# Starting addresses in SBUF: the buffers of the transposing DMAs move to multiples of 128 bytes

## The chip, the cores and the metric

The kernel runs on one core of one Trainium2 chip. The metric is device time in microseconds (us), the median of several runs of the whole program. The profile is of one further execution of it. The span is the time from the first to the last instruction in that execution.

## The reference: one hybrid encoder layer

The input `x` has 2048 tokens of width 1024, and there are 256 memory tokens. One layer is computed:

```
h    = rms_norm(x, norm_pre_w)
proj = h @ w_in          # aq (8 heads), ak, av (2 heads), bqkv, ba, bb, mq, z
y_a  = softmax attention of 8 query heads over 2 key/value heads, 2048 x 2048, 2-D rotary
y_b  = gated DeltaNet, forward and backward, 4 heads, after a short convolution
y_m  = softmax attention of 4 heads into the 256 memory tokens
mix  = concatenate([y_a, y_b, y_m]) * silu(z)
out  = x + rms_norm(mix @ w_out, norm_post_w)
```

All of it is float32 at the interface. The change concerns the softmax attention `y_a` and `y_m`: there, `P = softmax(scores)` has queries in the partitions and keys along the free axis, and the product `P @ V` needs `P` with keys in the partitions, so `P` is transposed.

## The kernel before

The work stands in stages that follow each other, with some overlap.

1. **Projections** (0 to about 880 us): weights are loaded through tiles called `wraw` and split into two fp16 parts, a high part and a remainder; the normalised tokens `hT` are kept in the same way. Queries, keys, values, gates and the DeltaNet inputs go to scratch tensors in HBM.
2. **DeltaNet scan** (about 880 to 1360 us): chunk by chunk, with gate projections as filler for TensorE.
3. **Attention** (about 1360 to 2310 us): 64 attention units of 256 queries of one head, each of two blocks of 128 queries, and 8 memory units of one block. That makes 136 blocks.
4. **Output projection** (about 2310 to 2650 us).

One attention block goes as follows. TensorE computes scores `sa` of 128 queries against 2048 keys, VectorE (DVE) takes their maximum `mxa`, ScalarE (ACT) exponentiates into `Pa`, and `high` and `low` make two fp16 parts of the scaled result side by side in one tile `hl` (named `hla` for attention blocks and `hlm` for memory blocks; 128 partitions by 8192 bytes, three buffers): the high part by ACT, the remainder by DVE for 1536 keys and by GpSimd (POOL) for 512. Then one DMA of 1 MB, issued on the queue of SyncE (SP), transposes `hl` into half of a tile `PT`, SBUF to SBUF. There are four `PT` tiles of 128 partitions by 16384 bytes, used in turn: `PT0` and `PT1` in the pool `hT`, `PT2` and `PT3` in the pool `late`. The value product `pva` (for memory units `pvm`) reads `PT` and `V` on TensorE. Its result is multiplied by a gate `gaa` that is loaded from HBM, and stored to `mix` in HBM.

The pool `hT` has six rooms of 16384 bytes per partition under the tag `B16`. In turn they hold `wraw`, `mT`, `hT0` to `hT3`, and later `K0`, `K1`, `V`, `M`, `PT0`, `PT1`, `mhl` and `wo`. The pools `wp`, `zp`, `at`, `bp`, `op` and those of the early stages lie behind it in SBUF, so that where `hT` ends sets where they begin. The pool `const`, which holds a few scale factors, lies before it.

During attention, ACT, DVE, TensorE and the sync queue run in the order in which the program was written. All loads and stores of this stage go through SP's queue, in one order with the transposes.

Of the kernel before, what the change touches and what calls it, by code (L numbers as in the profile page):

```python
# [11 lines left out]
F32 = mybir.dt.float32  # L12
F32R = mybir.dt.float32r
BF16 = mybir.dt.bfloat16
F16 = mybir.dt.float16
# [7 lines left out]
S = 2048  # L23
D = 1024
NMEM = 256
# [3 lines left out]
KC = D // 128  # L29
# [8 lines left out]
def hybrid_layer(ctx: ExitStack, tc: tile.TileContext, t: dict, out, dbg=None):  # L38
# [40 lines left out]
    const = ctx.enter_context(tc.tile_pool(name="const", bufs=1))  # L79
# [35 lines left out]
    ssq = const2.tile([128, 4, TB], F32, name="ssq")  # L115
    vmax = const2.tile([128, TB], F32, name="vmax")
    mvmax = const2.tile([128, 2], F32, name="mvmax")
    vs, vcs, mvs, mvcs, hs_, hcs = (const.tile([128, 1], F32, name=n) for n in ("vs", "vcs", "mvs", "mvcs", "hs", "hcs"))
    gcs = const.tile([128, 8], F32, name="gcs")
    gate_cs = [gcs[:, i:i + 1] for i in range(8)]  # L120

# [25 lines left out]
    def load_w(srcs, width, fac=(1.0,), fetch=None):  # L147


        n = wcount[0]  # L150
        wcount[0] += 1
        room = hpool.tile([128, 2, 4, width], F32, tag="B16", name="wraw", bufs=6)
        raws = [room[:, half] for half in range(2)]
        for half in range(2):
            for ap_to, ap_from in srcs(raws[half], half):
                (fetch or wdma)(ap_to, ap_from)
        pool, tag, bufs = (wpool, "whb", 2) if wpool is not None and n % 3 == 1 else (wp, "whl", 4)
        parts = [pool.tile([128, 2, 4, width], F16, tag=tag, name="wparts", bufs=bufs) for _ in range(2)]

        def small(name, dt=F32, pool=const2, bufs=4):  # L160
            return pool.tile([128, 1], dt, tag=name, name=f"{name}{n}", bufs=bufs)

        ss = [small(f"wss{i}") for i in range(2)]
        for half in range(2):
            A.activation(parts[half][:, 0].bitcast(BF16), raws[half], AF.Square, accum_out=ss[half])
        sb, y, e, sc = small("wsb", BF16), small("wy"), small("we", I32), small("wsc")
        V.tensor_tensor(sb, ss[0], ss[1], op=ALU.add)
        ps = tp_ps(f"wss{n}", (128, 1))
        T.matmul(ps, onesb, sb, start=True, stop=True)
        V.tensor_scalar(y.bitcast(I32), ps.bitcast(I32), -0.5, 1597463007.0, op0=ALU.mult, op1=ALU.add)  # L170
        V.tensor_scalar(e, y.bitcast(I32), 0x7f800000, None, op0=ALU.bitwise_and)
        V.tensor_scalar(sc.bitcast(I32), e, 1.0, float(14 << 23), op0=ALU.mult, op1=ALU.add)
        V.tensor_scalar(y.bitcast(I32), e, -1.0, float(240 << 23), op0=ALU.mult, op1=ALU.add)
        cs = [small("wc1", bufs=2)] * (len(fac) - 1) + [small("wc0", pool=const)]
        for c, f in zip(cs, fac):
            V.tensor_scalar(c, y, hcs, f, op0=ALU.mult, op1=ALU.mult)
        G.tensor_scalar(raws[1], raws[1], sc, None, op0=ALU.mult)
        A.activation(parts[0][:, 0], raws[0], AF.Copy, scale=sc)
        A.copy(parts[1][:, 0], raws[1])
        V.scalar_tensor_tensor(parts[0][:, 1], raws[0], sc, parts[0][:, 0], op0=ALU.mult, op1=ALU.subtract)  # L180
        G.tensor_tensor(parts[1][:, 1], raws[1], parts[1][:, 0], op=ALU.subtract)
        return [(w[:, 0], w[:, 1]) for w in parts], cs
# [3 lines left out]
    hpool = ctx.enter_context(tc.tile_pool(name="hT", bufs=1))  # L186
# [9 lines left out]
    def tp_ps(name, shape=(128, 512)):  # L196
        return ps1.tile(list(shape), F32, tag="tp", name=name, bufs=4)

    hT = []
# [48 lines left out]
    def load_group(segs, fetch=None, fac=(1.0,)):  # L248

        def src(raw, half):  # L250
            o = 0
            for c0, n in segs:
                yield raw[:, :, o:o + n], t["w_in"][0, 512 * half:512 * half + 512, c0:c0 + n].rearrange("(k p) c -> p k c", p=128)
                o += n
        return load_w(src, sum(n for _, n in segs), fac, fetch)
# [12 lines left out]
    with tc.tile_pool(name="s0", bufs=1) as p:  # L268
# [15 lines left out]

        wmem = p.tile([128, D], F32, tag="wn", name="wmem")
        wpre = p.tile([128, D], F32, tag="wn", name="wpre")
        mTt = hpool.tile([128, 2, KC, NMEM], F32R, tag="B16", name="mT", bufs=6)
        mT = [mTt[:, i] for i in range(2)]
        xs, hm = [], []
        for j in range(2):  # L290
# [58 lines left out]
        for g in range(4):  # L349
# [2 lines left out]
                wav, (avcs,) = load_group([(1280, 256), (3072, 16)], dma)  # L352
            mem_group(g, wg)
            wg = nxt
        hT.extend(hpool.tile([128, 2, KC, 512], F16, tag="B16", name=f"hT{b}", bufs=6).rearrange("p i k c -> i p k c") for b in range(4))
        hs = {}

        def tok_norm(tb):
# [285 lines left out]
                    (attention_loads, attention_slots)[b]()  # L644

    def slot(name, shape, dt=F32R):
        return hpool.tile(shape, dt, tag="B16", name=name, bufs=6)

    def late_slot(name, shape, dt=F32R):

        return late.tile(shape, dt, tag="L16", name=name, bufs=2)

    at = {}

    def attention_loads():

        at["k"] = [slot("K0", [128, 2, S])]
        at["q0"] = wp.tile([128, 2, QW], F32R, tag="wraw", name="qa0_0", bufs=1)
        dma(at["q0"], qT_d[0, :, :, 0:QW])
        for k in range(4):  # L660
            dma(at["k"][0][:, :, k * 512:(k + 1) * 512], kT_d[0, :, :, k * 512:(k + 1) * 512])

    def attention_slots():
        at["v"] = slot("V", [128, 2, TB, 256], F16)
        at["PT"] = [slot(f"PT{i}", [128, 2, 2, 16, 128], F16) for i in range(2)]
# [108 lines left out]
    with tc.tile_pool(name="s3a", bufs=1) as sv0:  # L774
        p = rows
# [24 lines left out]
        for hp in range(2):  # L800
            p = (sv0, sv1)[hp]
# [222 lines left out]
    late = ctx.enter_context(tc.tile_pool(name="late", bufs=1, side="right"))  # L1024
    ps2 = ctx.enter_context(tc.tile_pool(name="ps2", bufs=1, space=PSUM))
    p5 = ExitStack()
    p = p5.enter_context(tc.tile_pool(name="at", bufs=1))
# [7 lines left out]
    class Block:  # L1035
# [62 lines left out]
            V.reciprocal(sm[:, 2:3], sm[:, 2:3])  # L1098

        def high(self):  # L1100
            hl = self.hl = p.tile([128, 2, S], F16, tag="hl", name=f"hl{self.nm}", bufs=3)
            P = self.P.rearrange("p a c -> p (a c)")
            if self.u["mem"]:
                A.copy(hl[:, 0], P)
            else:
                A.activation(hl[:, 0], P, AF.Copy, scale=self.sm[:, 2:3])
            n = self.u["n"]
            if n in (2, 3) and len(PT) == n:
                PT.append(late_slot(f"PT{n}", [128, 2, 2, 16, 128], F16))
            self.pt = PT[n % 4][:, self.qb]  # L1110
# [136 lines left out]
    for i in range(len(blocks) + LAG + 1):  # L1247
# [31 lines left out]
        for tb in range(2):  # L1279
            n = i - len(blocks) - 2 * tb  # L1280
# [38 lines left out]
    with ExitStack() as es:  # L1319
        p = es.enter_context(tc.tile_pool(name="op", bufs=1))  # L1320
        wo.append([late_slot(f"wo{i}_2", [128, 4, D]) for i in range(2)])
        wo.append([p.tile([128, 4, D], F32R, name=f"wo{i}_3") for i in range(2)])

# [98 lines left out]
```

## Time and profile before

| | us |
|---|---|
| median of 3 runs (lowest to highest) | 2656.08 (2654.11 to 2661.66) |
| the profiled execution, its own time | 2652.8 |
| its span | 2650.6 |
| TensorE busy in the span | 2419.5 (91%) |
| VectorE busy | 1763.9 (67%) |
| ScalarE busy | 1258.9 (47%) |
| GpSimd busy | 691.4 (26%) |

The mean granted clock of TensorE is 0.975. The profiled execution is 3.3 us below the median of the runs, and 2.2 us of its time lie outside the span. Lines of the profile name an operation as output, an arrow, and inputs, without buffer numbers; nearly all operations have one source line, since a helper records them, so they are told apart by the names of tiles.

### The profile page before, as it was taken

Reading aid. Unit: us, or ns where it says so; the run is one execution under the profiler, and the core shown is the slowest. Engines: PE = TensorE matmul, PEld = TensorE weight load, DVE = VectorE, ACT = ScalarE, POOL = GpSimd, SP = SyncE. Lnnn points to the kernel's source line nnn. Section 1 sums busy time; section 2 is a strip of 40 time slices with the busy share of each in tenths; the row PEclk is TensorE's granted clock in tenths of the full one; section 3 lists DMA queues with packets and bytes.
Section 4 is the critical chain, followed back from the end, with each engine's and each line's share of the span. In section 5 each row is a group of like instructions: output and inputs, shape, how many; then the busy total and the mean of one; then the engine's idle time right before and its main releaser. Section 6 shows DMA issues by size and latency. Waiting matters only on the chain.

```text
span 2650.6 us, 43177 instructions
## 1 busy us (share of the span) xinstructions
PE 2419.5 (91%) x15970; PEld 1739.9 (66%) x15978; DVE 1763.9 (67%) x3423; ACT 1258.9 (47%) x2495; POOL 691.4 (26%) x572
## 2 busy tenths in 40 slices
PE   7899999999989899989997888888888988999998
PEld 6788965555544366666556666666666766788887
DVE  6677769999568545455447787777877877542222
ACT  4633335444432255555546666666666666421110
POOL 2154331111203210210214444344444333200000
PEclk9999999999999999999999999999999999999999
DMA  6433333234586667678669999999999999953331
GB/s 212 150 118 123 116 101 104 72 116 130 195 256 159 204 191 215 209 236 235 205 192 228 223 229 223 227 228 220 217 217 208 211 202 203 210 167 98 97 97 54
DMA packets 867730, 470.49 MB, mean 178 GB/s; under 512 B 640576, under 2 KB 809920, under 8 KB 867264
## 3 DMA queue, kind: packets, MB, share of 16 engines
q1 hardware_dynamic: 853792, 420.54, 65.7%
q0 software_dynamic: 13728, 47.19, 5.3%
q8 instruction: 126, 2.06, 0.3%
q14 instruction: 84, 0.69, 0.1%
HBM read 201.82 MB, written 123.21 MB: 123 GB/s over the span
## 4 chain that ended last, share of the span: by engine, by line
PE 26%; issue 11%; DMA 8%; POOL 8%; DVE 3%; ACT 1%; SPq 1%; POOLq 0%; DVEq 0%; ACTq 0%
PE o L51 12%; PE sa L51 4%; PE z L51 3%; POOL hla L51 3%; PE pva L51 3%; POOL Pa L51 2%; DMA PT<-hla 2%; DMA gaa<-gate 2%; POOL Pm L51 1%; DMA PT<-hlm 1%; PE pvm L51 1%; DVE mxa L51 1%; DMA xx<-bx 1%; DVE hla L51 1%; DMA n<-NI 1%
## 5 line engine op out<-in xcount | busy, mean ns | idle before, releaser
L51 PEld LDWEIGHTS <-wparts 128*128 128x128 f16 x3072 | 292.8, 98 | 326.8 <-issue 18.4
L51 PE MATMUL pva<-PT,V 128*128 128x256 f16 x3072 | 394.7, 280 | 97.6 <-DMA PT<-hla 91.1
L51 PE MATMUL sa<-K,qa 128*128 128x512 f32 x1536 | 435.3, 420 | 9.8 <-ACT Pm L51 5.1
L51 PEld LDWEIGHTS <-V 128*128 128x128 f16 x3072 | 287.3, 100 | 205.7 <-issue 109.6
L51 DVE TENSOR_REDUCE mxa<-sa 128x1 f32<-128x1024 f32 x256 | 309.6, 1217 | 138.2 <-PE sa L51 135.7
L51 ACT ACTIVATE Pa<-sa,mxa 128x1024 f32<-128x1024 f32 x256 | 282.6, 1110 | 242.0 <-DVE mxa L51 167.0
L51 PE MATMUL z<-hT,wparts 128*128 128x512 f16 x1536 | 371.9, 383 | 0.3
L51 PE MATMUL o<-wo,mhl 128*128 128x512 f32 x1416 | 325.1, 391 | 1.2 <-ACT wo L51 0.6
L51 PEld LDWEIGHTS sa<-K,qa 128*128 128x128 f32 x1536 | 281.6, 197 | 65.7 <-ACT Pm L51 6.5
L51 PEld LDWEIGHTS o<-wo,mhl 128*128 128x128 f32 x1416 | 265.3, 188 | 60.5 <-ACT wo L51 1.1
L51 DVE SCALAR_TENSOR_TENSOR hla<-Pa,sma,hla 128x1536 f16<-128x1536 f32 x128 | 284.5, 2222 | 14.8 <-ACT hla L51 14.5
L51 ACT ACTIVATE hla<-Pa,sma 128x2048 f16<-128x2048 f32 x128 | 256.1, 2001 | 58.7 <-DMA PT<-hla 50.1
L51 PE MATMUL b<-hT,wparts 128*128 128x512 f16 x1152 | 256.9, 379 | 0.5 <-ACT xb L51 0.5
L51 POOL TENSOR_TENSOR Pa<-Pa,sma 128x512 f32<-128x512 f32 x128 | 133.0, 1039 | 472.6 <-ACT hla L51 464.1
L51 PEld LDWEIGHTS <-hT 128*128 128x128 f16 x2304 | 227.0, 99 | 31.9 <-ACT hT L51 1.2
L51 PE MATMUL q<-wparts,hT 128*128 128x256 f16 x1920 | 215.6, 274 | 0.0
L51 POOL TENSOR_TENSOR hla<-Pa,hla 128x512 f16<-128x512 f32 x128 | 195.4, 1527 | 8.9
L51 POOL TENSOR_SCALAR wraw<-wraw,wsc 128x1024 f32<-128x1024 f32 (+1 forms) x22 | 68.1, 3097 | 335.7 <-DVE wy L51 224.1
L51 DVE TENSOR_TENSOR mhl<-mr,mhl 128x2048 fp32r<-128x2048 f32 (+1 forms) x16 | 35.1, 2192 | 179.7 <-ACT mhl L51 179.5
L51 DVE SCALAR_TENSOR_TENSOR y<-xb,convw,y 128x512 f32<-128x512 f32 x192 | 147.3, 782 | 1.5
L51 ACT CAST mhl<-mr 128x2048 fp32r<-128x2048 f32 (+1 forms) x16 | 29.2, 1825 | 228.3 <-PE o L51 214.4
L77 POOL DMA_DIRECT2D gate<-zg x64 | 35.5, 555 | 368.8 <-DVE zg L51 190.9
(302 smaller groups left out, 3244.3 us busy)
## 6 DMA issues: line engine op xcount, KB each, us to landing
xx<-bx SPq DMA_DIRECT2D x64, 512.0 KB, 4.8
wraw<-in_w_in POOLq DMA_DIRECT2D x42, 512.0 KB, 5.4
qT<-qo SPq DMA_DIRECT2D x32, 512.0 KB, 3.1
qa<-qT SPq DMA_DIRECT2D x64, 256.0 KB, 3.8
gate<-zg POOLq DMA_DIRECT2D x64, 256.0 KB, 4.0
NI<-nit SPq DMA_DIRECT2D x32, 512.0 KB, 3.5
mr<-mix SPq DMA_DIRECT2D x13, 1024.0 KB, 6.0
x<-in_x SPq DMA_DIRECT2D x16, 512.0 KB, 4.9
```

Of the source, the lines that this page charges most:

```text
L51: ins = f(*args, **kw)
L77: nc.gpsimd.dma_start(to, of)
```

## The change

The pools take an alignment for the tiles that share rooms with `PT` (the tag `B16`), for `late_slot`, and for `hl`. Six tiles of one float per partition in `const` become six columns of one tile.

```diff
-    vs, vcs, mvs, mvcs, hs_, hcs = (const.tile([128, 1], F32, name=n) for n in ("vs", "vcs", "mvs", "mvcs", "hs", "hcs"))
+    scales = const.tile([128, 6], F32, name="scales")
+    vs, vcs, mvs, mvcs, hs_, hcs = (scales[:, i:i + 1] for i in range(6))
 ...
-        room = hpool.tile([128, 2, 4, width], F32, tag="B16", name="wraw", bufs=6)
+        room = hpool.tile([128, 2, 4, width], F32, tag="B16", name="wraw", bufs=6, align_bytes=128)
 ...
-        mTt = hpool.tile([128, 2, KC, NMEM], F32R, tag="B16", name="mT", bufs=6)
+        mTt = hpool.tile([128, 2, KC, NMEM], F32R, tag="B16", name="mT", bufs=6, align_bytes=128)
 ...
-        hT.extend(hpool.tile([128, 2, KC, 512], F16, tag="B16", name=f"hT{b}", bufs=6).rearrange("p i k c -> i p k c") for b in range(4))
+        hT.extend(hpool.tile([128, 2, KC, 512], F16, tag="B16", name=f"hT{b}", bufs=6, align_bytes=128).rearrange("p i k c -> i p k c") for b in range(4))
 ...
-        return hpool.tile(shape, dt, tag="B16", name=name, bufs=6)
+        return hpool.tile(shape, dt, tag="B16", name=name, bufs=6, align_bytes=128)
 ...
-        return late.tile(shape, dt, tag="L16", name=name, bufs=2)
+        return late.tile(shape, dt, tag="L16", name=name, bufs=2, align_bytes=128)
 ...
-            hl = self.hl = p.tile([128, 2, S], F16, tag="hl", name=f"hl{self.nm}", bufs=3)
+            hl = self.hl = p.tile([128, 2, S], F16, tag="hl", name=f"hl{self.nm}", bufs=3, align_bytes=128)
```

What comes of it in the built program: every engine and every queue has the same instructions in the same order, with the same waits and the same semaphore updates; only the names of the six scale factors and the addresses differ. The addresses (bytes within a partition) go as follows; the last two columns give the place of the start behind the last multiple of 256.

| tiles | address before | after | before, mod 256 | after, mod 256 |
|---|---|---|---|---|
| `hl`, first of three buffers | 171744 | 171776 | 224 | 0 |
| `PT0` | 82464 | 82304 | 32 | 128 |
| `PT1` | 33312 | 33152 | 32 | 128 |
| `PT2` | 196576 | 196480 | 224 | 128 |
| `PT3` | 212960 | 212864 | 224 | 128 |
| `K0`, `K1`, `V`, `M`, `wraw`, `hT0` to `hT3` | -160 each | | 32 | 128 |
| `xx`, `it`, `gaa`, `qa`, `oo`, `zg` (pools behind `hT`) | -64 each | | 32 | 224 |
| `qo`, `mo` | -64 each | | 224 | 160 |
| `kt`, `sv` (in the DeltaNet inputs) | -64 each | | 96 | 32 |
| `ku` | -64 | | 32 | 224 |
| `nit` | 0 | | 96 | 96 |

The three `hl` buffers are 8192 bytes apart, and the halves of a `PT` tile too.

## Prediction

> **What bounds the kernel now.** I first read the busy time by stage (engines' busy time, then granted clock, DMA share, GB/s; the stages are those of the text above).
>
> ```profile
> core 0: us, PE busy (x) PEld busy (x) DVE busy (x) ACT busy (x) POOL busy (x), PEclk, DMA share, GB/s
> 1381.00:1900.00 519.00, 439.63 (x2807) 342.99 (x2805) 406.48 (x515) 332.80 (x479) 218.62 (x155) 0.95 1.11 224
> 1900.00:2310.00 410.00, 361.20 (x2267) 280.21 (x2266) 310.91 (x384) 255.85 (x300) 163.05 (x125) 0.96 1.08 209
> 2310.00:2650.00 340.00, 331.22 (x1444) 270.25 (x1442) 108.46 (x202) 51.38 (x56) 0.00 (x0) 1.00 0.34 107
> 0.00:1381.00 1381.00, 1287.45 (x9457) 846.41 (x9466) 938.01 (x2325) 618.84 (x1662) 309.73 (x293) 0.98 0.55 168
> ```
>
> Outside attention TensorE is busy 93% to 97% of the time, and no transposing DMA runs there. In attention (929 us, the first two rows) it is busy 800.8 us and idle 128. So 128 us is the most that anything done to the transposes could bring. Next, the answer on the tile `PT`: durations as least/median/greatest in ns, then who waits for it.
>
> ```profile
> L1122 SPq DMA_TRANSPOSE PT<-hla x128: 4685/5318/10240, 1381.1 to 2288.5; - x128
> L1122 SPq DMA_TRANSPOSE PT<-hlm x8: 4870/4964/5514, 1450.3 to 1878.2; - x8
> ...
> who waited for it (us, times):
>   PE pva L51: 91.1, 41
>   PEld L51: 85.8, 26
>   ACT hla L51: 52.3, 35
>   PE pvm L51: 19.2, 5
> ...
> DMA to landing us min/median/max: 6.7/7.4/12.3
> ```
>
> TensorE's matmuls wait 91.1 + 19.2 = 110.3 us for transposes, most of its idle time, in 46 of 136 cases. So the transposes do bound this stage, and the change is aimed at the right place. The question is what sets their pace. The first two rows are not the transfer: they are how long the issuing instruction holds SP's queue. At the medians that is 128 x 5.318 + 8 x 4.964 = 720 us of the 907 us between the first and the last. The order of time on SP's queue (start, duration) shows what fills the rest:
>
> ```profile
> 1756.28 6.25 SPq L1122 DMA_TRANSPOSE PT<-hla  x1
> 1762.58 4.95 SPq L1122 DMA_TRANSPOSE PT<-hlm  x1
> 1767.62 0.54 SPq L51 DMA_DIRECT2D mix<-gaa  x1
> 1768.26 4.90 SPq L1122 DMA_TRANSPOSE PT<-hla  x1
> 1773.26 0.55 SPq L51 DMA_DIRECT2D qa<-qT  x1
> 1773.91 4.96 SPq L1122 DMA_TRANSPOSE PT<-hla  x1
> ```
>
> Instructions stand with gaps of about 0.1 us. An ordinary load of the same 1 MB holds the queue for a thirteenth of that (row from the answer on `mr`, the output projection's input):
>
> ```profile
> L51 SPq DMA_DIRECT2D mr<-mix x16: 370/370/436, 2280.7 to 2580.6; - x16
> ```
>
> Is the hold the time that SP needs to issue the pieces, or is it held back by the transfer? If by the transfer, and if the transfer is slow because of its addresses, the change helps. Three short stretches inside single transposes tell this apart:
>
> ```profile
> 1406.90:1410.40 3.50, 3.50 (x28) 2.97 (x26) 2.62 (x6) 2.56 (x3) 1.85 (x2) 1.00 1.27 290
> 1491.90:1494.40 2.50, 2.50 (x19) 1.96 (x17) 1.94 (x5) 1.21 (x3) 0.56 (x1) 1.00 1.28 290
> 1764.00:1768.00 4.00, 4.00 (x31) 3.29 (x29) 3.15 (x5) 2.92 (x3) 1.00 (x1) 1.00 1.17 218
> ```
>
> The last is the ordinary pace, 218 GB/s: 1.0486 MB / 218 GB/s = 4.81 us, which is the hold of 4.685 to 4.96 us. The first two come late in transposes whose transfer was held up at its start while SP went on issuing; there the engines catch up at 290 GB/s, 3.62 us for 1 MB. Every `hl` buffer in this run starts at 224 behind a multiple of 256, these included. So the addresses of before allow 290 GB/s, and the ordinary 218 is set ahead of the data, at SP. How many pieces SP issues is shown by the packets of the stage:
>
> ```profile
> DMA packets 619683, 201.84 MB, mean 217 GB/s; under 512 B 565216, under 2 KB 617312, under 8 KB 619616
> ```
>
> Fewer than 565216 / 136 = 4156 pieces a transpose, so 4096 of 256 bytes make up the 1 MB: SP needs about 4.8 us / 4096 = 1.2 ns for each.
>
> **The change part by part.** *The transposes.* Source starts go from 224 to 0 behind a multiple of 256, destination starts from 32 (`PT0`, `PT1`) and 224 (`PT2`, `PT3`) to 128. The number of instructions, waits and pieces stays. Two prices are possible. If SP's issuing sets the hold, and a piece costs SP the same at any address, the gain is 0. If the address sets it, the bound on the other side is the pace of 290 GB/s or better: 4.81 - 3.62 = 1.19 us a transpose, 136 x 1.19 = 162 us of SP's time, more than the 110.3 us that TensorE waits, so all of these go and no more: -110.3. I take 0, since the stretches at 290 were reached with the old addresses. Where I am least sure is whether SP's 1.2 ns a piece itself depends on the address; no row shows a transpose at another source start, so the lower end stays.
>
> The Trainium skill, page "DMA: Bandwidth & Descriptors", section "How a descriptor splits into AXI transactions", speaks for a gain: a read starts at the 256-byte boundary below its start, and the bytes fetched ahead of it still cost beats of 32 bytes. By that a piece of 256 bytes at 224 costs 8 + 7 = 15 beats and an aligned one 8; with the 435 GB/s that the same page's specifications give as the fabric's ceiling, this would allow, as an estimate, 435 x 8 / 15 = 232 GB/s before. The ordinary 218 would fit; the 290 of the two stretches does not, so here the measurement decides against it. The sum by that rule would be -110.3 instead of 0.
>
> *The other rooms of `hT`* (`wraw`, `K`, `V`, `M`, `hT0` to `hT3`) go from 32 to 128, *and the tiles of the later pools* from 32 to 224 or from 224 to 160. Whether a plain DMA cares is bounded by transfers of equal size that start at different places before (size, us from issue to landing):
>
> ```profile
> qT<-qo SPq DMA_DIRECT2D x32, 512.0 KB, 3.1
> NI<-nit SPq DMA_DIRECT2D x32, 512.0 KB, 3.5
> bx<-kt SPq DMA_DIRECT2D x32, 256.0 KB, 2.3
> bx<-ku SPq DMA_DIRECT2D x16, 256.0 KB, 2.5
> ```
>
> The first pair starts at 224 and 96, the second at 96 and 32. The differences are 0.4 us in favour of 224 and 0.2 us against 32, with no order in them. All four are stores; they are the nearest rows, since the loads of these stages all start at 32. So the price of a move is between -0.4 and +0.4 us a transfer; I take 0, the middle, because the two pairs contradict each other. Where it would matter is where an engine waits for such loads (the waits: us in total, times, longest; behind them the loads, from the same view as the pairs above):
>
> ```profile
> DVE xx L51 <- DMA xx<-bx: 76.6, 47, 3.3
> DVE gaa L51 <- DMA gaa<-gate: 31.9, 15, 5.5
> ```
>
> ```profile
> xx<-bx SPq DMA_DIRECT2D x64, 512.0 KB, 4.8
> gaa<-gate SPq DMA_DIRECT2D x64, 128.0 KB, 3.7
> ```
>
> These are 47 + 15 = 62 waits, and both tiles go from 32 to 224: 62 x 0.4 = 25 us either way at the most.
>
> *The scale factors.* Six tiles become columns 4 bytes apart. Same writes, same reads, same waits: 0, with nothing that has to cover it. *Engines reading moved tiles:* matmuls on `PT` and the writers of `hl` keep shape and order. Half of the value products of before read a `PT` that starts at 32 and half one at 224 (`pvm` likewise), and they show no two prices: the median lies within 4 ns of the least.
>
> ```profile
> L51 PE MATMUL pva<-PT,V x3072: 269/273/437, 1397.9 to 2305.1; 128*128 128x256 f16 x192
> L51 PE MATMUL pvm<-PT,mv x192: 272/273/437, 1457.0 to 1890.5; 128*128 128x256 f16 x192
> ```
>
> I take 0 there; if each of the 3264 moved by 1 ns, the next whole number of the record, it would be 3 us either way.
>
> The sum is 0, with unknowns of -110.3 (transposes), +-25 (plain DMAs) and +-3 (matmuls). On the profiled execution that gives 2652.8 us. The median of the three runs is 3.3 us above it, and the change is measured against such medians, so I forecast 2656 us. A change of 0.3%, 8 us, is about what a measurement of this kernel can tell from none: the three runs differ by 7.6.
>
> **The rivals.** *A, the address sets the pace after all.* The hold then falls from 4.8 to 3.6 us or lower, SP's queue is free for a sixth of the stage, and the 110.3 us of waits go: 2656 - 110 = 2546 us; next late would be `mxa` waiting for `sa`, that is TensorE itself. For it: hold and transfer are nearly equal in length, and the order of the queue is packed. Against: 290 GB/s with the old addresses. The rule of the Trainium skill told above, from its page "DMA: Bandwidth & Descriptors", would lead to this case.
>
> *B, only the tail shrinks.* The median hold of 5.318 lies above the least, 4.685, since transposes run into transfers ahead of them. If aligned reads clear these faster, so that the hold falls to its least value, 0.63 us a transpose, it counts where TensorE waits: 46 x 0.63 = 29 us, so 2627 us. For it: the DMA share of 1.08 to 1.11 in the stage, so that engines are rarely idle. Against: the share counts overlapping packets (1.28 at 290 GB/s, 1.17 at 218), so that it shows no queue.
>
> *C, slower: the tiles pushed to 224 load later.* 62 waits on `xx` and `gaa` grow by up to 0.4 us: 2656 + 25 = 2681 us. It decides, against no change, from 8 / 62 = 0.13 us a transfer on. For it: loads of `xx` and `gaa` end waits of DVE on the path. Against: the store that starts at 224 (`qo`) is the quicker of its pair.
>
> **How the numbers follow.** No change 0.54; A 0.18 (the source of every transpose moves, and the stage is bound by them, but the rates contradict it); B 0.15; C 0.13. B and A end faster, C slower: faster 0.33, same 0.54, slower 0.13. The likeliest case alone lies in 2648 to 2664. The range for 8 in 10 must reach B on one side and into C on the other, and leaves A out: 2590 (between A and B, since a smaller part of A is as likely as all of it) to 2672 (C at two thirds of its price).
>
> **What would show it.** In the profile after, the row of `PT<-hla` should again have 4.7 and 5.3 us as least and median, with TensorE's waits near 110 us, and the window's GB/s near 217. A least hold below 4.5 us would show A; a median near 4.7 with the same least, B. Landings of `xx` (4.8 us) and `gaa` (3.7) up by over 0.13 us would show C. The forecast is wrong first of all if SP's time for a piece depends on where it starts.

## The result and the profile after

The changed kernel takes 2580.08 us (median of 4 runs, 2576.74 to 2586.11) against 2655.56 us of the kernel before (the three runs of the table above and one more): a ratio of 0.9714, with a 95% interval of 0.969 to 0.9738. A run more than 1.5% above the fastest of its kernel is left out of the ratios; there is one such run here, in experiment 5. The forecast was 2656, so the kernel gained some 75 us that the forecast did not see, and the time lies below its range. The profiled execution has a span of 2576.6 us, 74.0 less than before.

Busy time by stage, in the columns shown before:

```profile
core 0: us, PE busy (x) PEld busy (x) DVE busy (x) ACT busy (x) POOL busy (x), PEclk, DMA share, GB/s
1383.00:1900.00 517.00, 459.26 (x2984) 360.07 (x2983) 440.39 (x548) 355.14 (x505) 244.72 (x167) 0.96 1.11 241
1900.00:2233.00 333.00, 322.88 (x2094) 253.54 (x2093) 288.57 (x349) 231.40 (x273) 149.87 (x114) 0.99 1.08 233
2233.00:2573.00 340.00, 333.14 (x1442) 271.25 (x1440) 108.79 (x203) 51.40 (x56) 0.00 (x0) 0.99 0.33 105
0.00:1383.00 1383.00, 1286.28 (x9463) 844.92 (x9464) 937.15 (x2325) 618.43 (x1662) 308.84 (x293) 0.98 0.55 168
```

The stages ahead of and behind attention are as long as they were, within some 3 us. Attention went from 929 to 850 us, and TensorE's idle time in it from 128.2 to 67.9 us. Its busy time fell too, by 18.7 us to 782.1, at the same work: the granted clock of the two stretches rose from 0.95 and 0.96 to 0.96 and 0.99, which by itself gives some 14 us of it, as an estimate from clocks of two digits. Why the clock is higher no run here shows. So the 79 us of this stage are 60.3 of idle time and 18.7 of busy time.

The answer on the tile `PT`:

```profile
L1123 SPq DMA_TRANSPOSE PT<-hla x128: 3927/4490/11106, 1383.7 to 2211.6; - x128
L1123 SPq DMA_TRANSPOSE PT<-hlm x8: 4107/4296/5380, 1450.2 to 1845.6; - x8
...
PE pva L51: 38.7, 22
...
PE pvm L51: 18.6, 6
...
DMA to landing us min/median/max: 5.5/6.9/13.2
```

The least hold of SP's queue went from 4.685 to 3.927 us, the median from 5.318 to 4.490, the least landing from 6.7 to 5.5. TensorE's waits for transposes went from 110.3 to 38.7 + 18.6 = 57.3 us. Those 53.0 us are most of the idle time that went. By the medians, 128 x 4.490 + 8 x 4.296 = 609 us of SP's queue are held, where it was 720.

Medians leave out the long holds. Added up over the traces, from the first to the last DMA instruction on SP's queue in this stage:

| SP's queue in attention, us | before | after |
|---|---|---|
| held by the 136 transposes | 748.3 | 658.6 |
| held by loads and stores | 134.8 | 132.9 |
| gaps below 0.5 us | 35.0 | 35.1 |
| gaps of 0.5 us and more | 3.6 | 16.2 |
| together | 921.7 | 842.8 |

The queue is full in both kernels. The stage became shorter by what the transposes hold it less (89.7 us, 0.66 for each), less 12.6 us of new gaps.

### The profile page after: what moved, and what is told of

It is laid out like the page before. It is cut to its first block, busy times and chain, and to the rows that moved or that the text cites. A ratio compares the mean times of both kernels' runs of the same rounds, so it can differ in the third digit from the quotient of the medians.

```text
span 2576.6 us, 43185 instructions
## 1 busy us (share of the span) xinstructions
PE 2401.6 (93%) x15978; PEld 1729.8 (67%) x15978; DVE 1775.2 (69%) x3423; ACT 1256.4 (49%) x2495; POOL 703.4 (27%) x572
## 4 chain that ended last, share of the span: by engine, by line
PE 23%; issue 11%; POOL 10%; DMA 7%; DVE 2%; ACT 2%; SPq 1%; POOLq 0%; DVEq 0%; ACTq 0%
PE o L51 12%; POOL hla L51 5%; POOL Pa L51 3%; PE sa L51 3%; PE z L51 3%; PE pva L51 2%; POOL Pm L51 1%; DMA PT<-hlm 1%; DMA PT<-hla 1%; DMA xx<-bx 1%; PE pvm L51 1%; DVE hla L51 1%; DVE mxa L51 1%; DMA Od<-oo 1%; SPq L1123 1%
## 5 line engine op out<-in xcount | busy, mean ns | idle before, releaser
L51 PE MATMUL sa<-K,qa 128*128 128x512 f32 x1536 | 428.2, 414 | 5.9 <-ACT Pa L51 4.1
L51 PE MATMUL pva<-PT,V 128*128 128x256 f16 x3072 | 384.0, 276 | 44.6 <-DMA PT<-hla 38.7
L51 PEld LDWEIGHTS sa<-K,qa 128*128 128x128 f32 x1536 | 275.5, 192 | 59.7 <-ACT Pa L51 6.4
L51 DVE SCALAR_TENSOR_TENSOR hla<-Pa,sma,hla 128x1536 f16<-128x1536 f32 x128 | 293.8, 2296 | 12.1 <-ACT hla L51 11.8
L51 POOL TENSOR_TENSOR hla<-Pa,hla 128x512 f16<-128x512 f32 x128 | 206.8, 1616 | 8.9
L51 DVE TENSOR_TENSOR mhl<-mr,mhl 128x2048 fp32r<-128x2048 f32 (+1 forms) x16 | 35.1, 2192 | 181.4 <-ACT mhl L51 181.2
```

Of the source, the lines that this page charges most:

```text
L51: ins = f(*args, **kw)
```

## Experiment 1: which end of the transpose matters

Two kernels move one end each. The first is the kernel before with one edit:

```diff
-            hl = self.hl = p.tile([128, 2, S], F16, tag="hl", name=f"hl{self.nm}", bufs=3)
+            hl = self.hl = p.tile([128, 2, S], F16, tag="hl", name=f"hl{self.nm}", bufs=3, align_bytes=128)
```

It puts `hl` at 171776 as the change does, and leaves `PT`, `V`, `K`, `xx`, `gaa` and all other loaded tiles where they were; besides `hl` only `mxm` and `smm` move, small tiles of the memory units.

> The kernel before with hl alone moved to multiples of 256 (224 to 0); PT stays at 32 and 224, and all plain loads stay where they were. Theory 'read': the whole gain, 2580 us, least hold 3.9 us and median 4.5. Theory 'write': no change, 2656 us, least hold 4.7. Theory 'both ends': no change or a part of it. If the plain DMAs of the other moved tiles had made the gain (rival): 2656 us.

The second is the changed kernel with `hl` put back to 171744. The gap puts the whole pool `at` (`Pa`, `hl` and the small tiles beside them) back to its old place; all else stays moved:

```diff
     p = p5.enter_context(tc.tile_pool(name="at", bufs=1))
+    p.tile([128, 16], F32, name="gap")
...
-            hl = self.hl = p.tile([128, 2, S], F16, tag="hl", name=f"hl{self.nm}", bufs=3, align_bytes=128)
+            hl = self.hl = p.tile([128, 2, S], F16, tag="hl", name=f"hl{self.nm}", bufs=3)
```

> The changed kernel with hl put back to 224 behind a multiple of 256, by its old address, and everything else moved as in the change (PT at 128, V, K, M, wraw at 128, xx and gaa at 224). Theory 'read': no gain, 2656 us, least hold 4.7 us. Theory 'write': the whole gain, 2580 us, least hold 3.9. If the plain DMAs made the gain: 2580 us with a least hold still at 4.7.

Measured: source alone 2572.25 us, ratio 0.9706 (0.968 to 0.9733). The destinations and all other moves, with the source put back, 2652.09 us, ratio 0.9989 (0.9975 to 1.0003). From the answers on `PT`, the first kernel:

```profile
L1122 SPq DMA_TRANSPOSE PT<-hla x128: 3873/4470/10612, 1379.9 to 2203.5; - x128
...
PE pva L51: 35.7, 23
```

The second kernel:

```profile
L1124 SPq DMA_TRANSPOSE PT<-hla x128: 4727/5224/8984, 1386.7 to 2288.3; - x128
...
PE pva L51: 77.6, 33
```

The whole gain is in the source. Moving the destinations, and with them every tile of the pool `hT` and of the pools behind it other than `at`, is worth nothing that can be measured. The one-line version cannot be told from the change: the two intervals overlap.

## Experiment 2: a table of starting places

> This kernel computes no layer: it only copies x to the output, and before that issues transposing DMAs between buffers that start a chosen number of bytes behind a multiple of 256. Letters a to h stand for 0, 32, 64, ... 224, of source (src) and destination (dst). First part: groups of four 1 MB transposes back to back, twice each. Theory 'read' (the source's start sets the pace): with the destination at 0, holds of SP of about 3.9 us for the source at 0 and 4.7 to 4.9 us at 224, in between by how far a piece of 256 bytes reaches past the next multiple of 256 (least at 32, most at 224), and 3.9 us for every destination with the source at 0. Theory 'write': the other way round, 3.9 us for all sources, 4.7 us for destinations off a multiple of 64. Theory 'both ends': slow as soon as either is off. Second part: transposes of a quarter of the size (1024 pieces) and of full size, each alone, and each behind a plain load of 4 MB in the same queue. Theory 'issue' (SP needs longer for a piece at some addresses, whatever the engines do): the quarter behind the load, whose pieces only pile up, still holds SP 1.2 us at 224 against 0.98 us at the aligned start. Theory 'transfer' (SP is held back by the engines): the quarter behind the load holds SP equally long at all starts, and the difference shows only where the engines drain.

The kernel ran once. The rows are holds of SP's queue in ns for a 1 MB transpose in a row of others. The letter behind `src` and `dst` is the start behind a multiple of 256: a 0, b 32, e 128, h 224; the medians for 64, 96, 160 and 192 lie between 4.92 and 4.95 us as source. First the source:

```profile
L29 SPq DMA_TRANSPOSE dsta<-srca x8: 4044/4125/4988, 4.5 to 430.5; - x8
L29 SPq DMA_TRANSPOSE dsta<-srcb x8: 4827/4921/4989, 22.1 to 449.6; - x8
L29 SPq DMA_TRANSPOSE dsta<-srce x8: 4865/4892/5007, 81.8 to 509.3; - x8
L29 SPq DMA_TRANSPOSE dsta<-srch x8: 4855/4968/5032, 141.6 to 569.1; - x8
```

Then the destination, with the source at 0:

```profile
L29 SPq DMA_TRANSPOSE dstb<-srca x8: 4018/4090/4224, 161.4 to 586.6; - x8
L29 SPq DMA_TRANSPOSE dste<-srca x8: 4044/4124/4216, 211.3 to 636.7; - x8
L29 SPq DMA_TRANSPOSE dsth<-srca x8: 4030/4087/4128, 261.0 to 686.1; - x8
```

The destination's start changes nothing. The source's start has two values: 4.1 us at a multiple of 256, and 4.9 us anywhere else, 128 included. There is no clear slope between 32 and 224: the medians lie within 0.08 us of each other, and each row's own spread is wider. A transpose moves its source in pieces of 256 bytes (4096 of them for 1 MB, by the packets), so what counts is whether a piece crosses a multiple of 256 at all, not by how much; theory "read" had the end right and the grading wrong.

Of the second part, a quarter of the size alone holds SP for 1.23 us at every start, so theory "issue" is out (the 0.98 us expected at the aligned start did not come either):

```profile
L46 SPq DMA_TRANSPOSE loneb<-srca x3: 1232/1232/1232, 967.2 to 1357.7; - x3
L46 SPq DMA_TRANSPOSE loneh<-srch x3: 1232/1233/1233, 921.0 to 1319.4; - x3
```

Behind the load it told little, since the load's own length sets the hold, with no order between the starts:

```profile
L46 SPq DMA_TRANSPOSE frontb<-srch x3: 7747/8223/11126, 879.4 to 1283.5; - x3
L46 SPq DMA_TRANSPOSE frontb<-srca x3: 7899/8235/10148, 971.5 to 1360.5; - x3
```

The Trainium skill's page "DMA: Bandwidth & Descriptors", section "How a descriptor splits into AXI transactions", grades the cost by beats: worked out by its rule, a piece of 256 bytes costs 9 beats at 32, 12 at 128 and 15 at 224. The table's medians for these are 4.921, 4.892 and 4.968 us. So the trace agrees that a crossing piece costs more, and not that the cost grows with the part behind the boundary. Counted in the transactions of that section of the Trainium skill, an aligned piece is one and every crossing piece two, and that count has no grading either.

## Experiment 3: a multiple of 128 that is not one of 256

The change asks for 128. That `hl` came to lie at a multiple of 256 was how the pools fell. The edits on the changed kernel (the other five alignments are taken out in the same way):

```diff
-            hl = self.hl = p.tile([128, 2, S], F16, tag="hl", name=f"hl{self.nm}", bufs=3, align_bytes=128)
+            hl = self.hl = p.tile([128, 2, S], F16, tag="hl", name=f"hl{self.nm}", bufs=3)
...
     p = p5.enter_context(tc.tile_pool(name="at", bufs=1))
+    p.tile([128, 16], F32, name="gap")
```

> No alignment is asked for; the scale factors are merged as in the change, and a gap of 64 bytes puts hl at 128 behind a multiple of 256, so that it starts at a multiple of 128 as the change's words ask, but not of 256. PT0, PT1, V, K, M start at 128 too, PT2 and PT3 at 224. Theory 'a piece of 256 bytes must not cross a multiple of 256' (from the table, where 128 was as slow as 32 or 224): no gain, 2654 us, least hold 4.7 to 4.8 us, median 5.2. Theory 'a multiple of 128 is enough': 2575 us, least hold 3.9.

Measured: 2651.79 us, ratio 0.9983 (0.9967 to 0.9998).

```profile
L1124 SPq DMA_TRANSPOSE PT<-hla x128: 4695/5303/8653, 1383.3 to 2286.7; - x128
```

The hold is that of the kernel before. With `hl` at a multiple of 128, and `PT0`, `PT1`, `V` and `K` as well, there is no gain that can be told from none.

## Experiment 4: where the time is lost

The kernel before moved 290 GB/s in short stretches with its source at 224, and 218 otherwise. If a crossing piece were slow to move, 290 should not be possible.

> This kernel computes no layer: it copies x to the output at its end, and before that issues transposing DMAs from a source that starts at a multiple of 256 (named even) or 224 behind one (odd), to a destination at a multiple of 256. Part one: single transposes of 256 to 4096 pieces (a to g: 256, 512, 1024, 1536, 2048, 3072, 4096). Part two: 4096 pieces behind a plain load of 0.5, 1, 2 and 4 MB in the same queue (p to s). Part three: five transposes of 4096 pieces in a row behind a load of 4 MB (row). Theory 'ahead' (pieces are made ready ahead of the data movement at 290 GB/s for even and 218 for odd sources; the movement itself does 290 for both): SP is held equally by even and odd up to some number of pieces, then longer by odd; behind a load, odd transposes move at 290 GB/s as long as pieces have piled up, and the longer the load, the longer; in the row of odd ones the pace falls back to 218 GB/s after the first one or two, and the holds of the last three are 4.9 us, while even ones hold 4.1. Theory 'in step' (the movement itself slows when the 16 engines start together, and not when a load has put them out of step): the pace behind a load is 290 GB/s for all five odd transposes of the row, holds 4.1 us, and the length of the load matters little. If SP's own pace depended on the start: odd quarters would hold SP longer than even ones, which the table did not show.

The kernel ran once, and every row is three transposes. Holds of single transposes, nothing else in flight (b to g: 512, 1024, 1536, 2048, 3072, 4096 pieces). Source at a multiple of 256:

```profile
L40 SPq DMA_TRANSPOSE loneevenb<-srca x3: 1190/1190/1190, 20.8 to 438.3; - x3
L40 SPq DMA_TRANSPOSE loneevenc<-srca x3: 1232/1232/1232, 25.6 to 443.1; - x3
L40 SPq DMA_TRANSPOSE loneevene<-srca x3: 1317/1317/1608, 38.3 to 455.8; - x3
L40 SPq DMA_TRANSPOSE loneeveng<-srca x3: 3970/4006/4055, 56.4 to 473.8; - x3
```

Source at 224:

```profile
L40 SPq DMA_TRANSPOSE loneoddb<-srch x3: 1190/1190/1191, 23.1 to 440.6; - x3
L40 SPq DMA_TRANSPOSE loneoddc<-srch x3: 1232/1232/1232, 28.4 to 445.8; - x3
L40 SPq DMA_TRANSPOSE loneodde<-srch x3: 1788/1948/1950, 42.0 to 459.4; - x3
L40 SPq DMA_TRANSPOSE loneoddg<-srch x3: 4836/4843/4874, 62.0 to 479.4; - x3
```

Up to 1024 pieces both hold SP equally long, and from 512 to 1024 pieces the hold grows by 42 ns, 0.08 ns a piece. So SP itself is not slower at 224, and not the limit of either: the 1.2 ns a piece of the prediction is not SP's own time. At 2048 pieces the aligned transpose still follows this slope in two of three cases (1317), while the one at 224 is held to 1948; at 4096 both are held back by something behind SP, and the one at 224 longer. At 3072 it is 3029 against 3644.

What moved in stretches inside single transposes (GB/s at the end of a line): 1024 pieces at 224 and aligned, then 4096 pieces at 224 and aligned.

```profile
core 0: us, DVE busy (x) POOL busy (x), PEclk, DMA share, GB/s
29.60:30.80 1.20, 0.00 (x0) 0.00 (x0) 1.00 1.10 204
26.90:27.60 0.70, 0.00 (x0) 0.00 (x0) 1.00 1.26 287
64.00:67.00 3.00, 0.00 (x0) 0.00 (x0) 1.00 1.17 217
58.00:60.00 2.00, 0.00 (x0) 0.00 (x0) 1.00 1.28 290
```

SP was through with the 1024 pieces at 29.6 and 26.8 us; during these holds 3 and 1 GB/s moved, and behind them the pieces moved at two paces. So it is not the handing over that sets the pace, and in the terms of theory "ahead" a piece that SP has handed over is not yet ready.

The 4096 pieces behind a load of 0.5 MB (p) and of 1 MB (q):

```profile
L40 SPq DMA_TRANSPOSE lateevenp<-srca x3: 4572/4624/4792, 68.6 to 486.1; - x3
L40 SPq DMA_TRANSPOSE lateevenq<-srca x3: 5882/5896/6336, 82.5 to 500.1; - x3
...
L40 SPq DMA_TRANSPOSE lateoddp<-srch x3: 5448/5727/5862, 75.1 to 492.2; - x3
L40 SPq DMA_TRANSPOSE lateoddq<-srch x3: 5817/6012/6180, 90.5 to 508.1; - x3
```

Behind the short load the crossing transpose (the one at 224) is 1.1 us slower by the median, and 0.8 alone; behind the longer one the two are 0.1 us apart. Inside the crossing ones, behind 0.5 MB and behind 1 MB:

```profile
78.00:80.00 2.00, 0.00 (x0) 0.00 (x0) 1.00 1.19 218
95.00:97.00 2.00, 0.00 (x0) 0.00 (x0) 1.00 1.27 286
```

Behind 2 MB the crossing one holds SP even 1.3 us less (8542 against 9798 ns), which no theory expected and which stays unexplained; behind 4 MB the two are 0.1 us apart.

The five transposes in a row behind a load of 4 MB, source at 224 (the load keeps the pieces of the first one waiting for about 13 us):

```profile
L40 SPq DMA_TRANSPOSE rowodda<-srch x3: 14827/15033/15052, 187.6 to 605.8; - x3
L40 SPq DMA_TRANSPOSE rowoddb<-srch x3: 4894/4986/5027, 202.7 to 620.7; - x3
L40 SPq DMA_TRANSPOSE rowodde<-srch x3: 4920/5002/5029, 217.6 to 635.8; - x3
```

And what moved in stretches inside the first, second, third and last of them, and, in the last line, inside the fourth of the row with the source at a multiple of 256 (GB/s at the end of a line):

```profile
201.20:203.70 2.50, 0.00 (x0) 0.00 (x0) 1.00 1.27 290
204.60:208.00 3.40, 0.00 (x0) 0.00 (x0) 1.00 1.17 218
209.50:213.00 3.50, 0.00 (x0) 0.00 (x0) 1.00 1.16 216
219.50:222.00 2.50, 0.00 (x0) 0.00 (x0) 1.00 1.17 217
176.80:179.50 2.70, 0.00 (x0) 0.00 (x0) 1.00 1.24 284
```

The first moves at 290 GB/s, the later ones at 216 to 218, with holds of 4.9 to 5.0 us. That is what theory "ahead" expects: pieces become ready at about 217 GB/s if they cross a multiple of 256, they are moved at up to 290 whatever their start, and the higher pace lasts while pieces have piled up. Theory "in step" expected 290 throughout the row, and the length of the load to matter little. Of "ahead", that a longer load brings the higher pace shows between 0.5 MB (218) and 1 MB (286); beyond that the whole transpose is already fast.

What stays open is which part makes the pieces ready. It lies behind SP's instruction and ahead of the movement that the packets record; whether it fetches, splits or reads ahead, no view of these runs tells.

## Experiment 5: freeing the queue further

If SP's queue still bounds attention, loads taken off it should help. This is the one-line version of experiment 1 with one more edit:

```diff
-        dma(q, qT_d[h, :, :, q0:q0 + QW])
+        wdma(q, qT_d[h, :, :, q0:q0 + QW])
```

> hl alone at a multiple of 256, as in the earlier experiment on the source, and the 63 loads of queries (qa) issued from GpSimd instead of SP. SP's queue would be free of 63 holds of 0.55 us, 35 us. Theory 'SP's queue still bounds the stage': some 15 to 30 us below 2572, so about 2550. Theory 'TensorE and the chain through ACT and GpSimd bound it now': within 8 us of 2572, or slower, if the loads come late behind GpSimd's work on hl.

Measured: 2596.99, 2616.94 and 2625.37 us, and 2644.04 in the run that is left out; ratio 0.9837 (0.9783 to 0.9891), against 0.9706 without the edit, so it is slower by more than the intervals. "Or slower" was expected with the loads late behind GpSimd's work; in part it is GpSimd's work that comes late behind the loads. From the waits, and from the answer on `PT`:

```profile
POOL qa L77 <- PE sa L51: 218.2, 52, 13.1
```

```profile
L1122 SPq DMA_TRANSPOSE PT<-hla x128: 3875/4406/14200, 1385.2 to 2259.6; - x128
...
PE pva L51: 81.5, 21
...
PE pvm L51: 10.0, 4
```

A load of queries waits until TensorE has read the buffer that it refills. GpSimd's instructions stand in the order of the program, so that its part of `hl` comes behind this wait, and the transpose behind that. Issuing the 63 loads also takes GpSimd 0.745 us each by the median, 47 us in all; the run does not separate the two. TensorE waits 81.5 + 10.0 = 91.5 us for transposes again, though their least hold is as short as with the aligned source.

Added up as in the table above, SP's queue is spared 46.1 us of loads and stores against the one-line version (88.2 for 134.3). But its gaps of 0.5 us and more go from 14.6 to 78.5 us, and the transposes hold it for 700.0 us where it was 652.6. Of the gaps, 32.8 us end with GpSimd's work on `Pa` and `hl` (8.8 without the edit), and 35.6 stand ahead of stores to `mix` that wait for the gated result or for an earlier store. So late work of GpSimd is a part of it; the longer holds and the late stores are not explained. The one-line version itself has those 14.6 us of gaps in 837.5 us, so that SP's queue is still nearly full after the change; whether freeing it by another way would pay is not tried.

## Why the prediction was wrong

- *What bounds the kernel* held. Attention was the stage, the transposes what TensorE waited for there, and SP's packed queue the reason: the table of the queue has 3.6 us of longer gaps in 921.7. Nothing was won outside.
- *The price of the transposes* failed. "I take 0, since the stretches at 290 were reached with the old addresses" took the highest pace seen for the pace that sets the time. The row in experiment 4 shows what such a stretch is: pieces made ready while the engines were kept waiting. The ordinary 218 was set upstream, as the prediction said, but upstream depends on the address (experiment 2: 4.9 us at 224, 4.1 at a multiple of 256), which it named as its least sure point and then priced at nothing. In place of 0 the runs have 0.66 us a transpose in the mean, 89.7 us of SP's queue.
- *"At SP"* failed too: SP's own time is the same at both starts up to 1024 pieces, so that the 1.2 ns a piece are set by what takes the pieces from SP.
- *Rival A* had the mechanism and the direction, and its condition came true (a least hold below 4.5 us). Its price was too high: all 110.3 us of waits were to go, and 53.0 went. It took 1.19 us off a hold, from 290 GB/s, where the mean hold lost 0.66, and it priced the gain by the waits of TensorE. Priced by the full queue, 136 x 0.66 less the new gaps comes near the 79 us of the stage. The median hold, 4.490 us against 4.1 in the table's rows, fits with transposes that still run into other transfers; 28 waits are left. The 18.7 us of busy time that went with a higher granted clock were in no term. Together with some 7 us of other idle time, and some 5 us lost in the neighbouring stages, that makes the 74.
- *The rule of the Trainium skill* was weighed against a stretch that could not refute it. That rule (page "DMA: Bandwidth & Descriptors", the section named above) had the right sign; its grading by beats is not seen here.
- *Plain DMAs, matmuls and scale factors* at 0 held: 0.9989 with all of these moved but the pool `at`, and the source put back. Rival C is out; `xx` lands in 4.9 us (4.8 before) and `gaa` in 3.7 as before. VectorE's waits for `xx` did grow, from 76.6 to 89.6 us, but not by the start: they are 75.7 in the second kernel of experiment 1 with `xx` at 224, and 88.4 in experiment 5 with `xx` at 32. Its waits for `gaa` fell, from 31.9 to 6.9. The landings after the change:

```profile
xx<-bx SPq DMA_DIRECT2D x64, 512.0 KB, 4.9
gaa<-gate SPq DMA_DIRECT2D x64, 128.0 KB, 3.7
```

- *Rival B* fails as a mechanism: the least hold itself fell, by 0.76 us, and the median by as much (0.83).

## What to carry to other kernels

Where the pieces of a transposing DMA are 256 bytes, as here, start its source at a multiple of 256 bytes in SBUF, and ask for 256, not 128: a 1 MB transpose then holds its queue for 4.1 us instead of 4.9, and the destination may start at any of the tried places. A burst above the ordinary pace says that the moving part can go faster, not that the addresses are harmless; what feeds it has to be measured by itself, in a row long enough to use up what has piled up. Where an in-order queue is full, price a shorter hold by the sum of the queue, and not by the waits of the engine behind it alone. Where an alignment seems to work, look at the address that came of it before the rule is written down.

## What the runs showed of the hardware

A transposing DMA whose 256-byte source pieces cross a multiple of 256 runs at 216 to 218 GB/s, one whose pieces do not at 284 to 290 (4.1 us a hold against 4.9 in a row), with no clear grading between 32 and 224 bytes, and with no effect of the destination's start. SP hands over 1024 pieces in 1.23 us at either start, ahead of their movement; they then move at 204 GB/s (crossing) or 287. Crossing pieces that have waited behind a load of 1 MB or more move at 286 to 290. Plain loads and stores whose tiles moved from 32 to 224, from 32 to 128 or from 224 to 160 showed no difference in a whole kernel (0.9989, 0.9975 to 1.0003). Of the tiles in the table of addresses only `hl` came to a multiple of 256, so what such a start is worth to a plain DMA is not shown.
